# One plain feed-forward tile becomes a pair, and the second norm moves ahead of the first silu

## The chip, the core and the metric

The kernel runs on one core of a Trainium2 chip. The metric is device time in microseconds of one execution. The profile's times (us) count from the first instruction. TensorE is PE, VectorE is DVE, ScalarE is ACT, GpSimd is POOL, and SP issues most of the loads.

## The reference

One layer of a decoder for 512 prompt positions and 8 single sampled tokens, which the kernel treats as 520 columns. Cut to the part that matters:

```
x  = x + g1 * (merged @ w_out)
h2 = rms_norm(x, norm2_w) * (1 + sc2) + sh2        # mean over 1024 features, eps 1e-6
a, b = split(h2 @ w_ffn_in, 2)                     # 1024 -> 2 * 2816 (22 tiles of 128 each)
x  = x + g2 * ((silu(a) * b) @ w_ffn_out)
```

Everything is float32. Ahead of this lie a first norm, one large projection, dilated attention, a gating unit and the merge.

## The kernel before

**Layout.** Features lie on the partitions, the 520 columns on the free axis. The columns are worked on in two halves of 260. Every float32 weight tile of 128 x 1024 is split into a rounded part `hi` (an ACT copy, line 69) and a rest `lo` (a DVE subtraction, line 70), and so are the activations. A product of a weight tile with one half of the columns is 8 x 3 = 24 matmuls (`mm3`, lines 91 to 93) into one PSUM buffer of four (pool `pm`).

**Order.** The work is a list of jobs (`job`, `second_use`, `pair_job`). After each job's matmuls are written, `run` advances the side tasks by one step (`tick`, line 108: norms, sums, constants, each a generator whose `yield n` waits n ticks) and then prepares one weight tile, three tiles ahead. That order is a priority: a planner with a cost of its own for each instruction then places the instructions on each engine's queue. `behind(ins)` keeps an instruction behind a given one on its engine's queue. On the chip each engine works through its queue in that order.

**The second norm.** The last projection (`out_job`, matrix `wout`) runs over the first half's eight tiles and then the second's. `norm2(half)` squares each finished tile on ACT and adds the squares on POOL (the last on DVE). Then a matmul with ones (line 317) puts the sum over the features on every partition, and `rsqrt` computes the root with a mean on DVE (`ms`, line 878), Ln and Exp on ACT (lines 206 and 207) and three DVE steps (208 to 210), the last of which gives `rstd`. `modulate` makes from each feature tile the parts hi and lo of h2 (ACT line 296, DVE lines 294 and 297) and a whole copy for the sums (ACT line 300). The first half's norm runs beside the second half's projection, the second half's beside the first feed-forward products.

**The feed-forward tiles.** Of 22 tiles of the first feed-forward matrix, tiles 0 to 3 (`NPRE = 4`) are plain: each is four products (matrices a and b, first and second half of the columns), 96 matmuls. All the first-half products come first, then the second-half ones in the order 0, 2, 3, 1. The split weights of tiles 0, 2 and 3 are kept from the first half to the second: three of the six in a pool of their own (`khi`, `klo`, `KEPT_HOME`), three in the three ring buffers through which all weights go (`KEPT_RING`), which so prepare no other tile until their second use. Tile 1 is loaded and split twice. The silu of matrix a goes from PSUM to SBUF on ACT (line 946), and DVE multiplies it with the product of matrix b (line 949).

Tiles 4 to 21 are pairs (`pair_job`): the products of matrices a and b with both column halves are formed with seven block products of 12 matmuls (lines 994 to 996) in place of eight, 84 in all. This needs sums and differences of quarters of h2 and of the weights. `sums()` computes those of h2 on DVE (line 966, four steps), waits until the kept pool is released, and then splits three of them into the tile `tt` (line 969 on ACT, 966 on DVE). The fourth is split when the first pair runs.

**Tables.** ACT holds one set of functions at a time. `log_exp()` (line 200) asks for the set with Ln and Exp; a silu after it needs another load.

Of the kernel before, what the change touches and what calls it, by code (L numbers as in the profile page):

```python
# [13 lines left out]
AF = mybir.ActivationFunctionType  # L14
ALU = mybir.AluOpType
AX = mybir.AxisListType

P = 128
# [3 lines left out]
HT = 260  # L22
KD = 8
NFF = 22
EPS = 1e-6
# [7 lines left out]
def hybrid_layer(ctx: ExitStack, tc: tile.TileContext, io: dict):  # L33
    nc = tc.nc
    dve, act, pe, pool, sp = nc.vector, nc.scalar, nc.tensor, nc.gpsimd, nc.sync
# [13 lines left out]
    def slot(tag, name, dtype=F32, shape=(P, T)):  # L49
        return tp.tile(list(shape), dtype, tag=tag, name=name, bufs=BUFS[tag])  # L50
# [10 lines left out]
    def const(name, shape, src=None, eng=None, pl=None):  # L61
        t = (pl or cst).tile(list(shape), F32, tag=name, name=name)
        if src is not None:
            (eng or act).dma_start(out=t, in_=src)
        return t
# [17 lines left out]
    last_lo, last_mm = [None], [None]  # L83
# [107 lines left out]
    def behind(ins):  # L191

        return tc.issue_after(ins.ins) if ins else nullcontext()

    act_last = [None]
# [6 lines left out]
    def rsqrt(dst, a, tag, shape):  # L202

        y = slot(tag, "rs_y")[: shape[0], : shape[1]]
        t = slot(tag, "rs_t")[: shape[0], : shape[1]]
        act.activation(y, a, AF.Ln)
        act.activation(y, y, AF.Exp, scale=-0.5)
        dve.tensor_tensor(out=t, in0=y, in1=y, op=ALU.mult)
        dve.scalar_tensor_tensor(out=a, in0=t, scalar=-0.5, in1=a, op0=ALU.mult, op1=ALU.mult)
        return dve.scalar_tensor_tensor(out=dst, in0=a, scalar=1.5, in1=y, op0=ALU.add, op1=ALU.mult)  # L210


    cT = const("cT", (P, KD, 9), io["cT"], sp)
    ident = const("ident", (P, P))
    make_identity(nc, ident)
    ones = const("ones", (P, P))
# [164 lines left out]
    n2w = const("n2w", (P, KD))  # L381
# [13 lines left out]
    def late(out, src):  # L395

        with behind(after):
            sp.dma_start(out=out, in_=src)

    def constants():  # L400
        late(qw, io["qw"])
        late(kw, io["kw"])
        late(turns, io["turns"])
        late(lnw, io["lnw"].to_broadcast([P, 512]))
        late(lnb, io["lnb"].to_broadcast([P, 512]))
        yield 1
        with behind(last_h[0]):
            dve.tensor_scalar_mul(qw, qw, float(np.float32(128.0) ** -0.5))
        late(wsp, io["wspT"])
        late(tril, io["tril"])  # L410
        yield 3
        with behind(last_lo[0]):
            dve.tensor_tensor(out=wsp, in0=wsp, in1=tril.unsqueeze(1).to_broadcast([P, 8, P]), op=ALU.mult)
        late(bsp, io["bsp"])
        late(w00, io["w00"])
        yield 1
        late(bias0, io["bias0"])
        yield 1
        late(bias12, io["bias12"])
        late(n2w, io["n2w"])  # L420

    spawn(constants())


# [440 lines left out]
    def norm2(half):  # L865
        c = slice(half * HT, half * HT + HT)
        acc = slot("tr", "acc2", shape=(P, HT))
        for f in range(KD):
            sq = slot("tr", "sq2", shape=(P, HT)) if f else acc
            act.activation(sq, xr[f][:, c], AF.Square)  # L870
            if f:
                (pool if f + 1 < KD else dve).tensor_tensor(out=acc, in0=acc, in1=sq, op=ALU.add)
            yield 1
        tot = total(acc, "t")
        log_exp()
        rstd2 = slot("tr", "rstd2")
        ms2 = slot("tr", "ms2")
        dve.tensor_scalar(ms2[:, c], tot, 1.0 / 1024, EPS, op0=ALU.mult, op1=ALU.add)
        rsqrt(rstd2[:, c], ms2[:, c], "tr", (P, HT))
        yield 1  # L880
        if half == 0:
            h2_all.append(slots("h", "h2", 2 * KD, F32R))
            mem["ys"] = slots("ys", "g8")
            h2.extend((h2_all[0][1][f], h2_all[0][1][KD + f]) for f in range(KD))
            scales(1, 0, KD, n2w)
        else:
            modulate_samples(1, 0, KD, xr_all[0][0], rstd2, h2_all[0][0], mem["ys"][0])
        for f in range(KD):
            modulate(1, f, xr[f], rstd2, half * HT, min(half * HT + HT, TP), *h2[f],
                     mem["ys"][1][f])  # L890
            if f % 2:
                yield 1
        if half:
            spawn(sums(), 0)
# [38 lines left out]
    def ffn_job(i, which, half, place=None):  # L933

        def fn(hi=None, lo=None):
            if half == 0 and place:
                kept.halves[i, which] = hi, lo
            elif place:
                hi, lo = kept.halves.pop((i, which))
            p = product(hi, lo, h2, half)  # L940
            if half and place == "home" and not kept.halves.keys() & set(KEPT_HOME):
                kept.stack.close()
                kept.closed = True
            if which == 0:
                pend[i] = slot("tr", "silu", shape=(P, HT))
                act_last[0] = act.activation(pend[i], p, AF.Silu)
                return
            c = slice(half * HT, half * HT + HT)
            dve.tensor_tensor(out=home(i)[:, c], in0=p, in1=pend[i], op=ALU.mult)

        if half and place:
            second_use(fn, place == "ring")
        else:
            job(io["wff"][which * NFF + i], fn, home=keep if place == "home" else None, again=(place == "ring"))
# [5 lines left out]
    def sums():  # L960

        b = mem["ys"][0]
        b11, b12, b21, b22 = b[:, 0:4, 0:HT], b[:, 0:4, HT:T], b[:, 4:8, 0:HT], b[:, 4:8, HT:T]

        def minus(out, x, y):
            dve.tensor_tensor(out=out, in0=x, in1=y, op=ALU.subtract)

        def halved(hi, lo, src):
            act.activation(hi, src, AF.Copy)
            minus(lo, src, hi.bitcast(F32))  # L970


        for step in (lambda: minus(b11, b12, b11), lambda: minus(b12, b22, b12), lambda: minus(b22, b22, b11),
                     lambda: minus(b21, b21, b22)):
            with behind(last_lo[0]):
                step()
            yield 1
        while not kept.closed:
            yield 1
        tt = ctx.enter_context(tc.tile_pool(name="tt", bufs=1)).tile([P, 3, KD, HT], F32R, tag="tt", name="tt")  # L980
        mem["tt"] = tt
        for j, t in ((0, b22), (1, b12), (2, b21)):
            with behind(last_lo[0]):
                halved(tt[:, j, 0:4], tt[:, j, 4:8], t)
            yield 1
        h = h2_all[0][0]
        mem["t1"] = lambda: halved(h[:, 0:4, HT:T], h[:, KD : KD + 4, HT:T], b11)
# [124 lines left out]
                chain_[1] = dve.tensor_tensor(out=hl[1], in0=gs[k], in1=hl[0].bitcast(F32), op=ALU.subtract)  # L1112
            halved[k] = hl

    NPRE = 4
    KEPT_HOME = [(0, 0), (0, 1), (NPRE - 2, 0)]
    KEPT_RING = [(NPRE - 2, 1), (NPRE - 1, 0), (NPRE - 1, 1)]
    for half, tiles in ((0, range(NPRE)), (1, [0, NPRE - 2, NPRE - 1, *range(1, NPRE - 2)])):
# [143 lines left out]
```

## Time and profile before

| | us |
|---|---|
| median of three runs | 933.11 (932.98 to 933.7) |
| the profiled execution | 932.99 |
| its span, first to last instruction | 931.1 |
| PE busy | 909.2 (98%), 7636 matmuls |
| DVE busy | 580.4 (62%) |
| ACT busy | 414.8 (45%) |
| POOL busy | 137.6 (15%) |

The last projection's second half ends at about 571 us, the plain tiles run from 567.3 to 618.6, the pairs from there to some 800, and the down projection ends the kernel. A matmul's own record lasts about 0.28 us, as neighbours overlap; the distance between two starts is its cost. In a timeline row the bracket gives the engine's idle time before the instruction and what ended it.

### The profile page before, as it was taken

The numbers are of one execution on the slowest core, as the hardware profiler recorded it, in microseconds if no ns is written. First come the engines' busy times: TensorE is split into PE (matmuls) and PEld (weight loads), VectorE is DVE, ScalarE is ACT, GpSimd is POOL, SyncE is SP. The second block draws the span as 40 slices with busy tenths as digits, with TensorE's granted clock in tenths as the row PEclk, the third lists the DMA queues.
The fourth block names the chain that finished last, engine by engine and source line by source line (L and its number), as shares of the span: only waits on it lengthen the run. The fifth ranks groups of instructions, "written<-read, shape, count | busy, mean of one in ns | idle before, by whom it ended". The sixth has DMA issues, their size and how long they took to land.

```text
span 931.1 us, 18828 instructions
## 1 busy us (share of the span) xinstructions
PE 909.2 (98%) x7636; PEld 869.0 (93%) x7636; DVE 580.4 (62%) x1376; ACT 414.8 (45%) x818; POOL 137.6 (15%) x157
## 2 busy tenths in 40 slices
PE   3999999999999999999999999999999999999998
PEld 1799889899898989999999999999999999999998
DVE  6734675746755665643337768897888888842321
ACT  5343443443543443763333447655555555722110
POOL 0000002112102102201000322123233341000000
PEclk9999999999999999999999999999999999999999
DMA  9944436829758726645222556122332332343410
GB/s 357 361 166 132 164 114 226 272 83 309 249 178 235 244 90 176 222 129 162 92 91 92 207 180 203 47 92 92 108 121 91 98 130 92 105 146 92 126 35 24
DMA packets 41878, 142.66 MB, mean 153 GB/s; under 512 B 6328, under 2 KB 7320, under 8 KB 41792
## 3 DMA queue, kind: packets, MB, share of 16 engines
q1 hardware_dynamic: 32688, 110.14, 35.0%
q0 software_dynamic: 8608, 31.20, 11.0%
q8 instruction: 60, 0.98, 0.5%
q14 instruction: 26, 0.21, 0.1%
q10 hardware_dynamic: 496, 0.12, 0.1%
HBM read 132.81 MB, written 8.63 MB: 152 GB/s over the span
## 4 chain that ended last, share of the span: by engine, by line
PE 91%; DVE 3%; DMA 2%; ACT 2%; issue 1%; ACTq 0%; DVEq 0%; SPq 0%
PE ps L91 21%; PE ps L92 20%; PE ps L93 20%; PE pa L994 4%; PE pa L995 4%; PE pa L996 4%; PE ada L259 2%; PE pb L996 2%; PE pb L995 2%; PE pb L994 2%; PE y L672 1%; DMA wada<-wada 1%; PE ssq L524 1%; DVE lo L70 1%; PE p L996 1%
## 5 line engine op out<-in xcount | busy, mean ns | idle before, releaser
L91 PE MATMUL ps<-h,hi 128*128 128x260 f32 x1168 | 333.2, 288 | 4.0 <-ACT h L296 1.6
L93 PE MATMUL ps<-h,lo 128*128 128x260 f32 x1168 | 331.6, 285 | 0.5 <-DVE lo L70 0.5
L92 PE MATMUL ps<-h,hi 128*128 128x260 f32 x1168 | 331.3, 284 | 0.0
L70 DVE TENSOR_TENSOR lo<-raw,hi 128x1024 fp32r<-128x1024 f32 (+2 forms) x205 | 207.7, 1030 | 160.9 <-ACT hi L69 158.4
L69 ACT ACTIVATE hi<-raw 128x1024 fp32r<-128x1024 f32 (+2 forms) x205 | 170.7, 857 | 232.0 <-PE ps L92 203.1
L91 PEld LDWEIGHTS ps<-h,hi 128*128 128x128 f32 x1168 | 219.0, 189 | 16.0 <-issue 9.4
L93 PEld LDWEIGHTS ps<-h,lo 128*128 128x128 f32 x1168 | 220.3, 189 | 2.8 <-issue 1.7
L92 PEld LDWEIGHTS ps<-h,hi 128*128 128x128 f32 x1168 | 220.0, 188 | 2.8 <-issue 2.1
L1016 POOL TENSOR_TENSOR s<-raw 128x512 f32<-128x512 f32 x18 | 34.7, 1928 | 138.7 <-DMA raw<-wff 112.0
L995 PE MATMUL pb<-h,hi 128*128 128x260 f32 x144 | 40.8, 283 | 0.1
L994 PE MATMUL pa<-tt,hi 128*128 128x260 f32 x144 | 40.8, 283 | 0.1
L995 PE MATMUL pa<-tt,hi 128*128 128x260 f32 x144 | 40.8, 283 | 0.0
L996 PE MATMUL pb<-h,lo 128*128 128x260 f32 x144 | 40.8, 283 | 0.0
L994 PE MATMUL pb<-h,hi 128*128 128x260 f32 x144 | 40.7, 282 | 0.0
L996 PE MATMUL pa<-tt,lo 128*128 128x260 f32 x144 | 40.6, 282 | 0.0
L93 PE MATMUL ps<-mh,lo 128*128 128x260 f32 x128 | 36.4, 285 | 0.0
L91 PE MATMUL ps<-mh,hi 128*128 128x260 f32 x128 | 36.3, 284 | 0.0
L91 PE MATMUL ps<-gh,hi 128*128 128x260 f32 x128 | 36.3, 284 | 0.0
L92 PE MATMUL ps<-ml,hi 128*128 128x260 f32 x128 | 36.2, 283 | 0.0
L92 PE MATMUL ps<-gh,hi 128*128 128x260 f32 x128 | 36.1, 282 | 0.0
L93 PE MATMUL ps<-gh,lo 128*128 128x260 f32 x128 | 36.0, 282 | 0.0
L858 DVE SCALAR_TENSOR_TENSOR xr<-ps,mod,xr 128x260 f32<-128x260 f32 (+1 forms) x32 | 15.4, 483 | 30.7 <-PE ps L93 29.9
(280 smaller groups left out, 2000.4 us busy)
## 6 DMA issues: line engine op xcount, KB each, us to landing
raw<-win SPq DMA_DIRECT2D x60, 512.0 KB, 6.3
wada<-wada SPq DMA_DIRECT2D x48, 512.0 KB, 7.1
raw<-wff SPq DMA_DIRECT2D x46, 512.0 KB, 4.0
raw<-wout SPq DMA_DIRECT2D x16, 512.0 KB, 3.7
raw<-wfo SPq DMA_DIRECT2D x16, 512.0 KB, 3.8
kt<-ck POOLq DMA_DIRECT2D x8, 512.0 KB, 5.7
qb<-dq POOLq DMA_DIRECT2D x8, 512.0 KB, 5.5
raw<-wpj SPq DMA_DIRECT2D x8, 512.0 KB, 3.7
```

The source lines that it names most:

```text
L69: act.activation(hi, src, AF.Copy)
L70: return dve.tensor_tensor(out=lo, in0=src, in1=hi.bitcast(F32), op=ALU.subtract)
L91: pe.matmul(ps, wh, xh[:, cols], start=(first and i == 0), stop=False)
L92: pe.matmul(ps, wh, xl[:, cols], start=False, stop=False)
L93: last_mm[0] = pe.matmul(ps, wl, xh[:, cols], start=False, stop=(last and i == n - 1))
L259: last_ada[0] = pe.matmul(ps[32 * c : 32 * c + 32, :], cs[:, 4 * kh + c, :], w[:, c * 256 : c * 256 + 256], start=(kh == 0), stop=(kh == 1 ...
L524: pe.matmul(ssq[half][32 * g : 32 * g + 32, :], ones[:, 0:32], raws[g][1][:, c], start=True, stop=True, tile_position=(0, 32 * g))
L858: dve.scalar_tensor_tensor(out=dst[:, c0 : c0 + n], in0=ps[:, :n], scalar=g[:, 0:1], in1=x[:, c0 : c0 + n], op0=ALU.mult, op1=ALU.add)
L994: pe.matmul(ps, hi[:, c], xh, start=(first and k == 0), stop=False, skip_group_check=True)
L995: pe.matmul(ps, hi[:, c], xl, start=False, stop=False, skip_group_check=True)
L996: pe.matmul(ps, lo[:, c], xh, start=False, stop=(k == 3), skip_group_check=True)
L1016: pool.tensor_tensor(out=own_slot("s1", i % 2)[:, :512], in0=b[:, :512], in1=b[:, 512:], op=ALU.add)
```

## The change

`NPRE` falls from 4 to 3: tile 3 becomes the first of 19 pairs, and all six split weight tiles of tiles 0 to 2 are kept, so that none is loaded twice. A new function `rms` replaces `rsqrt` in the second norm: Ln reads the sum straight from PSUM, with scale 1/1024 and a constant bias of eps, the DVE step `ms` goes, and three DVE steps follow with a factor of -2048 left in the result, which the scaled `n2w` takes out. In the second half the sum is written with the last projection's tick, one tick earlier; every silu is queued behind the last Exp written; modulations come four to a tick, not two; and the four steps of the sums come two to a tick.

```diff
+    def rms(dst, tot, tag):
+        y = slot(tag, "rs_y", shape=(P, HT))
+        t = slot(tag, "rs_t", shape=(P, HT))
+        act.activation(y, tot, AF.Ln, scale=1.0 / 1024, bias=eps[:, 0:1])
+        exp_last[0] = act.activation(y, y, AF.Exp, scale=-0.5)
+        dve.tensor_tensor(out=t, in0=y, in1=y, op=ALU.mult)
+        dve.scalar_tensor_tensor(out=t, in0=tot, scalar=1024 * EPS, in1=t, op0=ALU.add, op1=ALU.mult)
+        return dve.scalar_tensor_tensor(out=dst, in0=t, scalar=-3072.0, in1=y, op0=ALU.add, op1=ALU.mult)
+    exp_last = [None]
...
+    eps = const("eps", (P, 1))
+    dve.memset(eps, EPS)
...
         late(n2w, io["n2w"])
+        yield 3
+        with behind(last_lo[0]):
+            dve.tensor_scalar_mul(n2w, n2w, -1.0 / 2048)
...
-            yield 1
+            if f + 1 < KD or half == 0:
+                yield 1
         tot = total(acc, "t")
         log_exp()
         rstd2 = slot("tr", "rstd2")
-        ms2 = slot("tr", "ms2")
-        dve.tensor_scalar(ms2[:, c], tot, 1.0 / 1024, EPS, op0=ALU.mult, op1=ALU.add)
-        rsqrt(rstd2[:, c], ms2[:, c], "tr", (P, HT))
+        rms(rstd2[:, c], tot, "tr")
...
-            if f % 2:
+            if f % 4 == 3:
                 yield 1
...
-                act_last[0] = act.activation(pend[i], p, AF.Silu)
+                with behind(exp_last[0]):
+                    act_last[0] = act.activation(pend[i], p, AF.Silu)
...
-        for step in (...):
+        for n, step in enumerate((...)):
             with behind(last_lo[0]):
                 step()
-            yield 1
+            if n % 2:
+                yield 1
...
-    NPRE = 4
+    NPRE = 3
     KEPT_HOME = [(0, 0), (0, 1), (NPRE - 2, 0)]
     KEPT_RING = [(NPRE - 2, 1), (NPRE - 1, 0), (NPRE - 1, 1)]
     for half, tiles in ((0, range(NPRE)), (1, [0, NPRE - 2, NPRE - 1, *range(1, NPRE - 2)])):
```

## Rows read from the trace of the kernel before

**Rows 1.** The page, busy time: us, share of the span, instructions.
```profile
PE 909.2 (98%) x7636; PEld 869.0 (93%) x7636; DVE 580.4 (62%) x1376; ACT 414.8 (45%) x818; POOL 137.6 (15%) x157
```

**Rows 2.** Busy us (instructions) by stretch: PE, PEld, DVE, ACT, POOL; clock, DMA share, GB/s.
```profile
550.00:560.00 10.00, 10.00 (x84) 9.94 (x84) 7.94 (x16) 5.91 (x10) 0.27 (x1) 1.00 0.54 166
560.00:580.00 20.00, 19.84 (x161) 19.25 (x160) 19.38 (x39) 14.38 (x28) 6.67 (x6) 1.00 0.68 224
580.00:590.00 10.00, 8.72 (x69) 8.33 (x68) 5.89 (x13) 7.61 (x10) 0.15 (x1) 1.00 0.28 87
580.00:620.00 40.00, 38.73 (x320) 38.33 (x319) 32.37 (x50) 25.60 (x46) 6.32 (x4) 1.00 0.16 56
700.00:750.00 50.00, 50.00 (x419) 50.00 (x418) 41.74 (x72) 27.72 (x56) 17.82 (x11) 1.00 0.32 106
```

**Rows 3.** Timeline of PE: start, us, line, operation, [idle before].
```profile
551.29 0.60 PE L317 MATMUL tot<-acc,ones 128*128 128x260 f32 x2
...
581.46 0.38 PE L317 MATMUL tot<-acc,ones 128*128 128x260 f32 x1
...
582.47 0.40 PE L91 MATMUL ps<-h,khi 128*128 128x260 f32 x1
...
588.25 0.28 PE L93 MATMUL ps<-h,lo 128*128 128x260 f32 x1
589.80 0.39 PE L91 MATMUL ps<-h,hi 128*128 128x260 f32 x1 [1.27 <-ACT silu L946]
```

**Rows 4.** Timeline of ACT, around both norms and the first pair.
```profile
553.30 0.40 ACT L206 ACTIVATE rs_y<-ms 128x260 f32<-128x260 f32 x1
...
560.51 0.50 ACT L296 ACTIVATE h<-modt,mod 128x260 fp32r<-128x260 f32 x1
...
582.03 0.39 ACT L946 ACTIVATE silu<-ps 128x260 f32<-128x260 f32 x1
582.43 1.28 ACT L200 ACT_TABLE_LOAD   x1
583.73 2.01 ACT L69 ACTIVATE hi<-raw 128x1024 fp32r<-128x1024 f32 x2
585.64 0.40 ACT L206 ACTIVATE rs_y<-ms 128x260 f32<-128x260 f32 x1
586.08 0.42 ACT L207 ACTIVATE rs_y<-rs_y 128x260 f32<-128x260 f32 x1
...
612.97 1.15 ACT L69 ACTIVATE hi<-raw 128x512 fp32r<-128x512 f32 x2 [1.54 <-PE ps L92]
```

**Rows 5.** Timeline of DVE, around both norms and the first pair.
```profile
551.92 0.43 DVE L878 TENSOR_SCALAR ms<-tot 128x260 f32<-128x260 f32 x1 [0.59 <-PE tot L317]
...
558.04 0.42 DVE L210 SCALAR_TENSOR_TENSOR rstd<-ms,rs_y 128x260 f32<-128x260 f32 x1
...
582.45 0.43 DVE L949 TENSOR_TENSOR g<-ps,silu 128x260 f32<-128x260 f32 x1 [2.40 <-PE ps L92]
...
588.02 0.43 DVE L210 SCALAR_TENSOR_TENSOR rstd<-ms,rs_y 128x260 f32<-128x260 f32 x1
...
598.90 0.47 DVE L297 SCALAR_TENSOR_TENSOR h<-modt,mod,h 128x252 fp32r<-128x252 f32 x1
...
605.91 2.39 DVE L966 TENSOR_TENSOR tt<-g,tt 128x1040 fp32r<-128x1040 f32 x2 [2.49 <-ACT tt L969]
...
613.63 2.39 DVE L70 TENSOR_TENSOR lo<-raw,hi 128x512 fp32r<-128x512 f32 x2
```

**Rows 6.** Groups of instructions in 580 to 620: busy us, mean ns | idle before.
```profile
L966 DVE TENSOR_TENSOR g<-g 128x1040 f32<-128x1040 f32 x4 | 4.9, 1237 | 0.1
L70 DVE TENSOR_TENSOR lo<-raw,hi 128x1024 fp32r<-128x1024 f32 x4 | 4.8, 1224 | 1.8 <-ACT hi L69 1.6
...
L69 ACT ACTIVATE hi<-raw 128x1024 fp32r<-128x1024 f32 x4 | 4.1, 1055 | 1.4 <-PE ps L92 1.4
```

**Rows 7.** Busy us (instructions) touching h2 alone, by stretch: PE, PEld, DVE, ACT; clock, DMA.
```profile
567.25:582.36 15.11, 12.34 (x96) 11.85 (x96) 2.41 (x5) 2.04 (x4) 1.00 0.56 181
```

More of the change, by code (lines that the diff above doesn't have):

```diff
@@ L970, in halved @@
             minus(lo, src, hi.bitcast(F32))
-        for step in (lambda: minus(b11, b12, b11), lambda: minus(b12, b22, b12), lambda: minus(b22, b22, b11),
-                     lambda: minus(b21, b21, b22)):
+        for n, step in enumerate((lambda: minus(b11, b12, b11), lambda: minus(b12, b22, b12),
+                                  lambda: minus(b22, b22, b11), lambda: minus(b21, b21, b22))):
             with behind(last_lo[0]):
                 step()
-            yield 1
+            if n % 2:
+                yield 1
         while not kept.closed:
```

## The prediction

> **What bounds the kernel now.** I read the page's first part, then busy time by stretch, then the PE, ACT and DVE timelines around the change. TensorE works for 98% of the span [rows 1] at the full granted clock. In the pair stage 419 matmuls start in 50 us [rows 2], one every 0.1193 us, and DVE, busy for 41.74 of those 50 us, keeps up. So time goes only where matmuls go, or where PE stands still. The one sizeable standstill near the change is in 580 to 590 us, where 69 matmuls start and 84 fit [rows 2]. It is one wait: a matmul at 588.25 us, the next at 589.80, released by a silu [rows 3].
>
> That silu was late because of ACT's tables. ACT runs the first silu at 582.03, goes back to the logarithm's table for the norm (582.43), makes two copies in 2.01 us, runs Ln and Exp, and then needs the silu table again [rows 4]: three table loads in 10 us, of which one row stands here. Four PSUM buffers hold the products, so PE cannot open another until a silu empties one.
>
> DVE is the second limit: it is busy for 7.94 us of 550 to 560, for 19.38 of 560 to 580, and for 32.37 of 580 to 620 [rows 2]. The second half of h2 is made there: its rstd begins at 588.02, its last piece at 598.90 [rows 5].
>
> **The change, part by part.** *One plain tile becomes a pair.* A plain tile costs 2 matrices x 2 halves x 24 = 96 matmuls, a pair 7 products x 12 = 84. Twelve fewer at 0.1193 us: -1.43 us, all on PE's path.
>
> It also removes four whole-tile splits from the stage before the pairs (tile 3's two and the repeated two of tile 1), ACT 1.05 and DVE 1.22 us each [rows 6], and two weight loads; the new pair's own work goes to the pair stage, whose DVE has 8.26 us left over per 50 [rows 2]. Worth nothing directly, as all this lies beside matmuls.
>
> *The stage before the pairs gets shorter.* It loses 96 matmuls, 11.5 us, while the second half's norm, modulation and the sums for the pairs stay. DVE idles 40.00 - 32.37 = 7.6 us in it now. It saves 4 x 1.22 + 2 x 0.43 (tile 3's two products with silu) + 0.43 (the ms step) = 6.2 us [rows 5, 6]. 7.6 + 6.2 - 11.5 leaves 2.3 us spare: the work fits, if its waits line up. Cost by this: 0 if they do, 2.6 us by the bound under rival 2; I take 0 because ring buffers still give each new tile two products (5.7 us) between its buffer's release and its use, and the first such split after the kept tiles shows no PE wait now.
>
> *Ln and Exp ahead of the first silu.* Two of three table loads go, the two copies of 2.01 us vanish with their tiles, and the standstill at 588.25 goes: 1.55 - 0.12 = -1.43 us [rows 3].
>
> What is late next is the first silu. Behind it stand the buffer of the first product, the later silus on ACT, and PE's fifth product. Now the fifth starts at 582.47, 0.05 us after that silu ended at 582.42 [rows 3, 4]; the four products before it ended their issue at about 582.38. In the new order the chain from the sum is: PE to reader 0.63 (551.29 to 551.92 [rows 3, 5]); Ln 0.44 (585.64 to 586.08), plus 0.10 for its bias operand (0.50 for a modulation with bias, 0.40 for Ln without [rows 4]); Exp 0.42; table 1.28; silu 0.39; hand-over 0.05. Together 3.3 us. The sum's matmul stands at 581.46, 0.92 us before 582.38. If it stays there, PE stands still 2.4 us.
>
> It should move up. In the first half, ms starts on DVE at 551.92, Ln only at 553.30 behind a weight copy, and rstd at 558.04 [rows 4, 5]. Without ms, Ln can start near 551.9, and rstd can be ready near 551.92 + 0.54 + 0.42 + 3 x 0.43 + 0.1 = 554.3, 4.1 us before its end at 558.47 now. The modulations that fill DVE in 560 to 580 [rows 2], now issued in two groups of four, can then use the 2.06 us that DVE idles in 550 to 560 [rows 2]; with ms gone, DVE should come to the last projection's residual, and through it to the sum, about 1.6 us earlier. That leaves 2.4 - 1.6 = 0.8 us of standstill. Bounds: 0 and 2.4; I take 0.8.
>
> The Trainium skill ("ScalarE: Activation LUTs", section "What ACT_TABLE_LOAD costs") charges a switch with a load of about 1283 ns and a drain of about 1380 ns. Here the silu ended at 582.42, the load began at 582.43, and the next copy at 583.73 [rows 4]: 1.30 us in all, no drain to be seen. By the page's figure the standstill would be 1.4 us more and the time about 932.6 (an estimate).
>
> *The sum with the last projection, four modulations at a time.* This fixes how early the second half of h2 is ready against its first reader. Let E be Exp's start. rstd is ready at E + 0.42 + 3 x 0.43 + 0.05, or E + 1.8. From rstd to the last piece took 598.90 + 0.47 - 588.45 = 10.9 us, with one 1.24 us sum step between [rows 5, 6]; without that step 9.7, so E + 11.5. PE resumes at E + 0.42 + 1.28 + 0.39 + 0.05 = E + 2.1, runs two products (48 x 0.1193 = 5.7) and reads the last piece 2.5 us into the next, at E + 10.4. So the last pieces are up to 1.1 us late. The cover is the next product's earlier pieces; PE's queue already crosses products over their pieces in the first half: the 96 matmuls of the first four products are spread over 15.11 us, among the last projection's [rows 7]. Bounds 0 and 1.1; I take 0.2, near the covered end.
>
> *Small edits.* The eps fill and the scaling of norm2's weights are single small DVE steps (a step of 260 columns takes 0.42 us, these have 1 and 8), the first before the first norm, the second in the stages where DVE has gaps: 0. Fewer yields in the sums change only the order. SP gains no DMA and loses two.
>
> **Sum.** -1.43 - 1.43 + 0.8 + 0.2 = -1.86 us. The profiled execution took 932.99 us (span 931.1 and 1.9 around it), the median is 933.11. 932.99 - 1.86 = 931.13; with the 0.12 to the median, 931.2.
>
> **Rivals.** *1. The first silu takes the place of the second as PE's wait.* If the instruction queues keep the sum at its place, because DVE spends the time won on weight splits (it is all but full over 560 to 580), the standstill is 2.4: -2.86 + 2.4 + 0.2 = -0.3, 932.8. For it: in the first half DVE now runs a weight split between the norm's own steps. Against it: the norm of the first half no longer passes through DVE before Ln. The table's longer price, above, belongs here as well, with 1 chance in 50.
>
> *2. Slower: DVE's waits do not fit in the shorter stage.* Place: from the sum to the first pair. DVE now waits 2.40 us for a product (582.45) and 2.49 for the copies of the transformed tiles (605.91) [rows 5]. These are dependences, not spare time. If both stay, 4.9 us of waits meet 2.3 us of spare, and 2.6 us of DVE work comes after PE wants it. A late DVE also leaves the sum where it is (2.4) and the last pieces late (1.1): -2.86 + 2.4 + 2.6 + 1.1 = +3.2, 936.3. It decides against the change from 2.9 us of new standstill on, and exceeds 0.2% from 4.7. For it: the spare is small. Against: both waits end with PE's products, and a shorter stage brings these forward too.
>
> *3. More gain.* The standstill at the first silu is 0, and PE's thin places (161 matmuls in 560 to 580 where 168 fit [rows 2]) close, since the first half's norm is early: 7 x 0.12 = 0.8 us, -2.86 - 0.8 = -3.7, 929.4. Against: those places follow weight splits, whose count there does not fall.
>
> *4. The kept halves do not do what they should.* All three ring buffers are held until the second halves, so the first pair's splits start no earlier than the first ring product ends. The first pair's first split took from 612.97 on ACT to 616.0 on DVE [rows 4, 5], 3.1 us of the 5.7 there are; with three ACT copies of about 1.05 [rows 6] ahead of it, 6.3. Price 0.6, time 931.8: inside the forecast's own range.
>
> **How the numbers follow.** Forecast (with rival 4) 50%, own range 930.0 to 932.2; rival 1 23%; rival 2 15%; rival 3 12%. Faster by over 0.2% (1.87 us, about what a measurement of this kernel can tell from no change) is 931.24 or less: a little over half of the forecast's chance, as its centre lies at that border, and rival 3: 0.41. Slower by over 0.2%: most of rival 2, which spreads from 933 up, and a rest: 0.14. Between: 0.45. The range goes from 929.4 (rival 3's time) to 934.6, which takes in rival 1 and the lower part of rival 2 and leaves out about 10% above and 5% below.
>
> **What would show it.** Right: one ACT table load between 575 and 600, Ln, Exp and then silu; no 1.5 us wait of PE after two products behind the first silu; instead a wait of 0.5 to 1.5 us ahead of the fifth product, released by silu; the first half's rstd at about 555; 12 matmuls fewer; the pair stage still at 0.1193 us. Wrong: a PE wait on pieces of h2 or on a split of the first pair longer than 1 us; more than 2 us at the first silu; a pair stage in which DVE is full.

## The result, and the profile after

The changed kernel takes 939.92 us in the median (938.73 to 940.74), the kernel before beside it on the same chip 933.6. The ratio is 1.0062, with an interval of 1.0051 to 1.0074: slower, and outside the predicted range of 929.4 to 934.6. The profiled execution took 938.78 us, its span is 937.0, against 932.99 and 931.1 before.

The page's first part for the changed kernel, busy us (share of the span) and instructions, answers to [rows 1]:

```profile
PE 909.7 (97%) x7624; PEld 869.3 (93%) x7624; DVE 582.2 (62%) x1384; ACT 413.0 (44%) x821; POOL 141.7 (15%) x159
```

The twelve matmuls are gone, as predicted, and yet PE's busy time has not fallen. Busy time by stretch tells why. The columns are those of [rows 2], and the last two rows are short stretches at the waits:

```profile
580.00:620.00 40.00, 37.22 (x284) 36.49 (x284) 32.14 (x56) 21.49 (x45) 6.00 (x6) 0.92 0.06 21
700.00:750.00 50.00, 50.00 (x419) 50.00 (x418) 41.97 (x70) 27.20 (x55) 17.95 (x10) 1.00 0.29 101
579.60:583.00 3.40, 3.33 (x14) 3.17 (x15) 3.40 (x5) 1.44 (x4) 3.40 (x4) 0.52 0.48 154
590.60:593.40 2.80, 2.80 (x13) 2.80 (x14) 2.80 (x9) 1.86 (x5) 0.00 (x0) 0.50 0.02 6
```

In 580 to 620 only 284 matmuls start, where 320 did before, and the granted clock is 0.92 of full speed. The loss sits at two waits of PE, each with a short stretch at about half clock, the 1.2 GHz level, behind it. The pair stage (700 to 750) is as before, to the matmul.

PE's timeline shows both (start, us, line, operation, [idle before <- what ended it]):

```profile
577.62 0.28 PE L91 MATMUL ps<-h,khi 128*128 128x260 f32 x1
579.67 0.54 PE L92 MATMUL ps<-h,khi 128*128 128x260 f32 x1 [1.77 <-DVE h L311]
...
583.05 0.34 PE L91 MATMUL ps<-h,khi 128*128 128x260 f32 x1
...
587.08 0.28 PE L93 MATMUL ps<-h,lo 128*128 128x260 f32 x1
587.20 0.60 PE L331 MATMUL tot<-acc,ones 128*128 128x260 f32 x2
590.58 0.59 PE L91 MATMUL ps<-h,hi 128*128 128x260 f32 x1 [2.78 <-ACT silu L963]
...
593.34 0.32 PE L91 MATMUL ps<-h,hi 128*128 128x260 f32 x1
...
597.82 0.39 PE L91 MATMUL ps<-h,khi 128*128 128x260 f32 x1
```

From the first matmul on h2 (568.71; 567.30 before) to the fifth product (590.58; 582.47 before) it takes 21.87 us, 6.70 more than before [rows 3, 7]. Three terms make it up. A wait of 2.05 us for a piece of h2: 1.93 over a normal step. Fourteen matmuls at half clock, 579.67 to 583.05: 3.38 - 14 x 0.1193 = 1.71. The wait for the first silu, 587.20 to 590.58 without the sum's own two passes of 0.12: 3.14. Together 6.78. Behind it twelve more matmuls run at half clock, 2.76 us for 1.43, so that the 1.43 which the old standstill gives back is not to be seen; the section on the clock asks what that stretch costs.

The balance is best made from the first matmul on h2 to the end of the span, 363.80 us before and 368.29 after, since single profiles reach that matmul anywhere between 567.2 and 570.1. Kernels with the same order of instructions ahead of it (the changed one and the one with PE kept busy, below) reach it at 568.71 and 570.06. The stage up to the first pair takes 46.35 instead of 51.34 - 11.45 (a plain tile), +6.46. The rest takes 321.94 instead of 312.46: 9.48 for a pair, 0.54 less than 84 x 0.1193. With the twelve matmuls, +6.46 - 0.54 - 1.43 = +4.49. The remaining 1.4 of the 5.9 between the two spans lie ahead of h2. They look like scatter: PE's order is the same with three and with four tiles in the new order up to 24 matmuls ahead of that one. But all nine profiles with three tiles reach it later (568.2 to 570.1) than four of the five with four tiles (567.2 to 567.9; the fifth 569.1), so whether a part belongs to the change stays open.

ACT's timeline shows that the new order did what it says, one table load in place of three:

```profile
587.89 0.48 ACT L216 ACTIVATE rs_y<-tot,eps 128x260 f32<-128x260 f32 x1 [2.50 <-PE tot L331]
588.40 0.42 ACT L217 ACTIVATE rs_y<-rs_y 128x260 f32<-128x260 f32 x1
588.84 1.28 ACT L963 ACT_TABLE_LOAD   x1
590.13 0.39 ACT L963 ACTIVATE silu<-ps 128x260 f32<-128x260 f32 x1
```

From the sum at 587.20 to PE's resumption is 3.38 us, a chain in which nothing waits. The prediction made it 3.3. It only began too late. Two things set its start: when the squares' sum `acc` is ready on DVE, and where the sum's matmul stands on PE's queue. In the kernel before the last addition on DVE was this one:

```profile
579.62 0.43 DVE L872 TENSOR_TENSOR acc<-acc,sq 128x260 f32<-128x260 f32 x1 [0.62 <-ACT sq L870]
```

It ended at 580.05, and the sum's matmul started at 581.46: with its operand ready, it stood 1.41 us in PE's queue (the shortest such distance in these runs is 0.21). In the changed kernel that addition (586.19, below) ends at 586.62, 17.9 us after the first matmul on h2 where before it took 12.75, and the matmul follows 0.58 us later, behind all 96 matmuls of the first four products.

POOL and DVE show the other half, the reason for the late operand: work that the prediction did not look for here. Their timelines, POOL first:

```profile
574.44 1.64 POOL L1034 TENSOR_TENSOR s<-raw 128x512 f32<-128x512 f32 x1 [4.34 <-DMA raw<-wff]
576.16 1.50 POOL L1035 TENSOR_TENSOR raw<-raw 128x512 f32<-128x512 f32 x1
577.63 1.71 POOL L889 TENSOR_TENSOR acc<-acc,sq 128x260 f32<-128x260 f32 x1
579.29 1.47 POOL L1034 TENSOR_TENSOR s<-raw 128x512 f32<-128x512 f32 x1
580.72 0.74 POOL L889 TENSOR_TENSOR acc<-acc,sq 128x260 f32<-128x260 f32 x1
581.41 1.46 POOL L1035 TENSOR_TENSOR raw<-raw 128x512 f32<-128x512 f32 x1
```

```profile
574.85 1.25 DVE L880 TENSOR_TENSOR xr<-rt,xr 128x8 f32<-128x8 f32 x1
...
576.43 0.47 DVE L875 SCALAR_TENSOR_TENSOR xr<-ps,mod,xr 128x252 f32<-128x252 f32 x1
576.82 1.92 DVE L70 TENSOR_TENSOR lo<-raw,hi 128x1024 fp32r<-128x1024 f32 x1
578.67 0.95 DVE L311 SCALAR_TENSOR_TENSOR h<-modt,mod,h 128x260 fp32r<-128x260 f32 x1
579.54 1.24 DVE L880 TENSOR_TENSOR xr<-rt,xr 128x8 f32<-128x8 f32 x1
580.71 1.04 DVE L311 SCALAR_TENSOR_TENSOR h<-modt,mod,h 128x260 fp32r<-128x260 f32 x1
581.74 1.42 DVE L311 SCALAR_TENSOR_TENSOR h<-modt,mod,h 128x260 fp32r<-128x260 f32 x1
...
586.19 0.43 DVE L889 TENSOR_TENSOR acc<-acc,sq 128x260 f32<-128x260 f32 x1 [0.64 <-POOL acc L889]
```

Lines 1034 and 1035 are the sums of the first two pairs' weight quarters. Before, the first of them ran at 589.85, after the norm. With one plain tile fewer the pairs' weights are loaded that much earlier, and POOL takes them up between the norm's own adds. Beside POOL's steps, DVE steps that read two operands from SBUF take longer: 0.95 to 1.42 us for 0.48, 1.92 for 1.21, 1.25 for 0.15. The step that reads one operand from PSUM (`xr<-ps`, 576.43) keeps its 0.47 beside POOL's second step.

### The profile page after: what moved, and what is told of

Its sections match the earlier page's. It is cut to its first block, busy times and chain, and to the rows that moved or that the text cites. A ratio compares the mean times of both kernels' runs of the same rounds, so it can differ in the third digit from the quotient of the medians.

```text
span 937.0 us, 18807 instructions
## 1 busy us (share of the span) xinstructions
PE 909.7 (97%) x7624; PEld 869.3 (93%) x7624; DVE 582.2 (62%) x1384; ACT 413.0 (44%) x821; POOL 141.7 (15%) x159
## 4 chain that ended last, share of the span: by engine, by line
PE 91%; DMA 3%; DVE 3%; ACT 1%; issue 1%; SPq 0%; DVEq 0%; ACTq 0%; POOLq 0%
PE ps L91 21%; PE ps L92 20%; PE ps L93 20%; PE pa L1013 4%; PE pa L1014 4%; PE pa L1012 4%; PE pb L1014 2%; PE pb L1013 2%; PE pb L1012 2%; PE ada L273 2%; PE y L689 1%; DMA wada<-wada 1%; PE ssq L541 1%; PE p L1013 1%; PE p L1014 1%; PE p L1012 1%
## 5 line engine op out<-in xcount | busy, mean ns | idle before, releaser
L91 PE MATMUL ps<-h,hi 128*128 128x260 f32 x1136 | 324.3, 288 | 5.8 <-ACT silu L963 2.8
L93 PE MATMUL ps<-h,lo 128*128 128x260 f32 x1136 | 322.4, 285 | 0.6 <-DVE lo L70 0.6
L92 PE MATMUL ps<-h,hi 128*128 128x260 f32 x1136 | 322.5, 285 | 0.3 <-DVE h L311 0.3
L70 DVE TENSOR_TENSOR lo<-raw,hi 128x1024 fp32r<-128x1024 f32 (+2 forms) x206 | 205.0, 1014 | 158.4 <-ACT hi L69 156.1
L91 PEld LDWEIGHTS ps<-h,hi 128*128 128x128 f32 x1136 | 213.5, 189 | 17.4 <-issue 9.1
L92 PEld LDWEIGHTS ps<-h,hi 128*128 128x128 f32 x1136 | 214.3, 189 | 3.3 <-issue 2.1
L93 PEld LDWEIGHTS ps<-h,lo 128*128 128x128 f32 x1136 | 214.4, 189 | 2.8 <-issue 1.7
L1034 POOL TENSOR_TENSOR s<-raw 128x512 f32<-128x512 f32 x19 | 37.6, 1981 | 144.3 <-DMA raw<-wff 104.4
L1013 PE MATMUL pa<-tt,hi 128*128 128x260 f32 x152 | 43.1, 283 | 0.0
L1014 PE MATMUL pb<-h,lo 128*128 128x260 f32 x152 | 43.0, 283 | 0.0
L1012 PE MATMUL pb<-h,hi 128*128 128x260 f32 x152 | 43.0, 283 | 0.0
L1012 PE MATMUL pa<-tt,hi 128*128 128x260 f32 x152 | 42.9, 283 | 0.0
L1013 PE MATMUL pb<-h,hi 128*128 128x260 f32 x152 | 42.9, 282 | 0.0
L1014 PE MATMUL pa<-tt,lo 128*128 128x260 f32 x152 | 42.8, 282 | 0.0
```

The costliest lines, as they stand in the source:

```text
L70: return dve.tensor_tensor(out=lo, in0=src, in1=hi.bitcast(F32), op=ALU.subtract)
L91: pe.matmul(ps, wh, xh[:, cols], start=(first and i == 0), stop=False)
L92: pe.matmul(ps, wh, xl[:, cols], start=False, stop=False)
L93: last_mm[0] = pe.matmul(ps, wl, xh[:, cols], start=False, stop=(last and i == n - 1))
L1012: pe.matmul(ps, hi[:, c], xh, start=(first and k == 0), stop=False, skip_group_check=True)
L1013: pe.matmul(ps, hi[:, c], xl, start=False, stop=False, skip_group_check=True)
```

## The experiments

Every ratio is to the kernel before on the same chip. The last column is the time from the first matmul on h2 to the end of the span, from one profile each (363.80 before, 368.29 after); that one execution can lie up to 3.5 us from the kernel's median (943.18 and 939.70 for the one with PE kept busy).

| kernel | ratio, interval | us |
|---|---|---|
| four tiles, old order | 0.9995, 0.9985 to 1.0006 | 363.74 |
| four tiles, new order | 1.0045, 1.0030 to 1.0061 | 368.41 |
| three tiles, old order | 1.0095, 1.0069 to 1.0120 | 373.67 |
| after: three tiles, new order | 1.0062, 1.0051 to 1.0074 | 368.29 |
| pairs' POOL sums behind the norm's adds | 1.0035, 1.0019 to 1.0051 | 368.35 |
| the same, early pair splits too | 1.0031, 1.0018 to 1.0044 | 366.24 |
| norm's second adds on DVE | 1.0054, 1.0036 to 1.0072 | 369.01 |
| before, with POOL steps added | 0.9994, 0.9983 to 1.0004 | 362.79 |
| PE kept busy at the silu | 1.0075, 1.0040 to 1.0109 | 371.34 |
| three tiles, silus copied out | 1.0048, 1.0029 to 1.0066 | 366.53 |
| four tiles, silus copied out, samples first | 1.0020, 1.0006 to 1.0033 | 364.75 |
| three tiles, silus copied out, samples first | 1.0062, 1.0045 to 1.0079 | 367.92 |
| the same, POOL sums last | 1.0022, 1.0012 to 1.0031 | 365.41 |

### The norm's new order, and the third tile, apart

The first kernel keeps the whole change but the tile; the second also takes back the sum's tick and the silus' place behind Exp; the third does that with three tiles.

```diff
-    NPRE = 3
+    NPRE = 4
```

> The changed kernel with four plain tiles as before: the norm's part of the change alone. Theory A: no pair's sum comes into the norm, since the pairs' weights come later; the wait of 1.43 us for the second silu goes, that at the first silu stands instead with 0 to 2.4 us: 932.5 to 934.5. Theory B: 2.4 us or more at the first silu, with the clock at half behind it: 935 to 937. Theory C says nothing of it: 932 to 934.

```diff
-            if f + 1 < KD or half == 0:
-                yield 1
+            yield 1
...
-                with behind(exp_last[0]):
-                    act_last[0] = act.activation(pend[i], p, AF.Silu)
+                act_last[0] = act.activation(pend[i], p, AF.Silu)
...
-    NPRE = 3
+    NPRE = 4
```

> Four plain tiles, the new rms and the modulations four at a time, but the sum is written one tick later as before and the silu is not queued behind Exp, so the first silu stands ahead of Ln and Exp again with three table loads. Theory B, the silu order, now put so: the sum's matmul comes only when TensorE has used up its four buffers, and the chain sum, Ln, Exp, table, silu of 3.3 us stands whole in TensorE's way, with a stretch at half clock behind it; then this run loses that wait, has the wait of about 1.4 us for the second silu in its place, and takes 933 to 934.5, some 4 us less than with the new order (937.97). Rival: the new rms or the grouping of the modulations is what costs; then it stays at 936.5 to 938.

> The changed kernel with three plain tiles, the sum written one tick later as before and the silu not queued behind Exp; the early GpSimd sums of the pairs stay. Theory B: the wait of 3.4 us ahead of the fifth product goes, a wait of 1.4 us or more for the second silu comes, and what the GpSimd sums cost stays: 936 to 938. Theory A alone (GpSimd's queue is the whole loss): 939 to 940.

Measured: the new order alone makes four tiles slower (1.0045), and taking it back gives the time of before (0.9995) with the new `rms` still in. So `rms`, its DVE step fewer and the regrouped modulations are worth nothing by themselves, and the order costs 4.7 us (0.0050 x 934); how much of it the tick costs and how much the silus' place is not shown. The third tile alone costs more still: 1.0095 against 0.9995, 9.3 us. The two costs overlap, since their sum is far more than the 5.8 of both (0.0062 x 934). Two of the three came out above all that was expected of them: the new order with four tiles at 937.97, three tiles in the old order at 942.46. PE's timeline of four tiles in the new order, and busy time in the stretch behind it:

```profile
581.98 0.60 PE L331 MATMUL tot<-acc,ones 128*128 128x260 f32 x2
582.22 0.47 PE L93 MATMUL ps<-h,lo 128*128 128x260 f32 x1
585.80 0.59 PE L91 MATMUL ps<-h,khi 128*128 128x260 f32 x1 [3.11 <-ACT silu L963]
```

```profile
585.80:590.90 5.10, 5.10 (x23) 5.10 (x24) 5.10 (x11) 2.99 (x8) 2.62 (x2) 0.50 0.24 90
```

The first POOL sum of a pair runs at 585.36 here, so it has no part in this wait. The squares' sum is ready on DVE at 580.22, and its matmul starts only at 581.98, with one matmul of the four products left. So PE stands still for 3.58 us behind the silu's chain (a weight copy stands ahead of Ln in it), with 24 matmuls at half clock behind that: 5.10 us, 2.2 too many. The same place in the old order, where the first silu ran at 581.16, ahead of Ln:

```profile
589.40 0.39 PE L91 MATMUL ps<-h,hi 128*128 128x260 f32 x1 [0.56 <-ACT silu L961]
596.16 0.39 PE L91 MATMUL ps<-h,khi 128*128 128x260 f32 x1 [0.72 <-ACT silu L961]
```

Three table loads and two waits of 0.85 and 1.00 us from start to start, none followed by a lower clock, cost far less than one open chain. With three tiles in the old order PE waits elsewhere:

```profile
582.02 0.39 PE L92 MATMUL ps<-h,khi 128*128 128x260 f32 x1 [1.75 <-DVE h L311]
584.15 0.59 PE L92 MATMUL ps<-h,khi 128*128 128x260 f32 x1 [0.77 <-DVE h L311]
...
602.42 0.80 PE L91 MATMUL ps<-h,khi 128*128 128x260 f32 x2 [4.40 <-ACT h L69]
```

The first two are pieces of h2's first half, delayed as in the changed kernel. The last are the samples' columns of its second half, which reach PE only after 4.68 us. The logarithm starts late (the sum at 594.29), and three tiles then leave too few products to cover the second half's norm. The new order, in which no wait of this length is left there, gains 3.1 us at three tiles.

### POOL's sums

First, the first two pairs' sums behind the norm's last POOL add:

```diff
+            with behind(last_add[0] if i < NPRE + 2 else None):
                 pool.tensor_tensor(out=own_slot("s1", i % 2)[:, :512], in0=b[:, :512], in1=b[:, 512:], op=ALU.add)
                 pool.tensor_tensor(out=b[:, :512], in0=a[:, :512], in1=b[:, :512], op=ALU.subtract)
```

> The changed kernel, but the GpSimd sums of the first two pairs' weights (two per pair) are queued behind the norm's last GpSimd addition. Theory A, GpSimd's queue: these four steps (1.64, 1.50, 1.47 and 1.46 us) stand between the additions of the second half's squares and also stretch VectorE's steps beside them; put behind, the wait of 2.05 us for a piece of h2 goes, the sum's matmul comes 4 to 5 us earlier, the wait at the first silu falls from 3.4 to under 1.5 us, and the time to about 934 (5 to 6 us less). Theory B, the silu order: the sum comes earlier but TensorE still waits 2.4 us or more for the first silu, and the time is 936 to 937. Theory C, the stage is too short for VectorE whatever the order: no change, 939 to 940.

DVE's timeline in the stretch in which its steps were long:

```profile
576.59 1.21 DVE L70 TENSOR_TENSOR lo<-raw,hi 128x1024 fp32r<-128x1024 f32 x1
577.73 0.48 DVE L311 SCALAR_TENSOR_TENSOR h<-modt,mod,h 128x260 fp32r<-128x260 f32 x1
578.13 0.71 DVE L880 TENSOR_TENSOR xr<-rt,xr 128x8 f32<-128x8 f32 x1
```

The steps have their length of before, the wait of 2.05 us and the half clock after it are gone, and the last matmul of the fourth product starts at 584.01, 3.5 us sooner when counted from the first matmul on h2. The silu's wait stays (584.13 to 587.46, then half clock). About 2 us of the median come back (937.82), less than either theory wanted. The profiled execution (939.61) shows little of it: the POOL sums now run from 582.35 to 588.4, and the two splits behind them (line 70, 583.85) take 3.42 us for what takes 1.36 at the free rate of 0.68, with a further wait of 2.25 us at 594.54.

Next, those splits too, behind Exp and DVE's last add:

```diff
+            with behind(exp_last[0] if early_pair else None), behind(last_add[1] if early_pair else None):
                 split(own_slot("ah", i % 2)[:, :512], own_slot("al", i % 2)[:, :512], b[:, 512:])
```

> As the run before, and the split of the fourth combination (ah, al) of the first two pairs is also queued behind the norm: its copy behind Exp, its subtraction behind VectorE's last addition. Theory A: the two subtractions (1.23 and 0.68 us) that stood ahead of the last residual step and of the last addition go, the sum comes another 1 to 1.5 us earlier, the time is about 933. Theory B: as the run before, 936. Theory C: 939 to 940.

Median much the same (936.98, 1.0031), and the silu's wait is now the largest single one, 583.83 to 588.19: the splits' two copies, put behind Exp, stand ahead of the table load on ACT (585.31 to 586.44). Next, POOL's sums left early and the second half's adds moved from POOL to DVE:

```diff
-                (pool if f + 1 < KD else dve).tensor_tensor(out=acc, in0=acc, in1=sq, op=ALU.add)
+                (pool if f + 1 < KD and half == 0 else dve).tensor_tensor(out=acc, in0=acc, in1=sq, op=ALU.add)
```

> The changed kernel, but all additions of the second half's squares run on VectorE; the pairs' GpSimd sums stay as early as they are. This parts the two ways in which GpSimd can hurt. If it is only that the additions wait in GpSimd's queue, the sum comes about 3 us earlier and the time is 935 to 936. If it is mostly that GpSimd's steps stretch VectorE's beside them, VectorE's steps between 575 and 584 us stay at twice their length, the wait of 2 us for a piece of h2 stays, and the time is 938 to 940. Theory C: 940 or more, for 5 x 0.43 us more on VectorE.

```profile
580.03 0.39 PE L92 MATMUL ps<-h,khi 128*128 128x260 f32 x1 [2.70 <-DVE h L311]
```

```profile
578.50 1.48 DVE L311 SCALAR_TENSOR_TENSOR h<-modt,mod,h 128x260 fp32r<-128x260 f32 x1
```

With nothing of the norm queued behind POOL's sums the wait for h2 stays, 2.98 us, DVE's step for that piece takes 1.48 us for 0.48, and the sum comes only 0.5 us earlier, counted from the first matmul on h2 (17.97 us for 18.48). So POOL hurts through DVE, and its queue is the smaller part. Last, the kernel before with eight unused POOL steps of 112 columns among the norm's adds:

```diff
+            for _ in range(2 if half and 2 <= f < 6 else 0):
+                pool.tensor_tensor(out=idle, in0=acc[:, :112], in1=acc[:, :112], op=ALU.add)
```

> The kernel before with nothing changed but eight additional POOL steps (112 columns each, their result unused), two behind each of four adds of the second half's norm, where in the changed kernel the pairs' POOL steps stand. DVE's and ACT's queues are as before. Theory A (POOL's steps delay the norm by themselves, through POOL's queue and by stretching DVE steps beside them): the eight take about 0.7 to 0.9 us each, the sum's matmul comes 2 us or more later than 581.46, DVE steps of 0.45 us beside them show 0.9 or more, PE waits 1 to 3 us more in 575 to 592, and the time is 934.5 to 937. Theory B (only the new order of table, Ln, Exp and silu costs time, POOL's steps lie beside matmuls): within 0.2% of before, 933 to 934.5.

The time is that of before. The sum comes 15.05 us after the first matmul on h2, 0.9 later than before, and not the 2 that the first theory wanted. In the old order silu does not hang on it, and PE's wait for the second silu even falls from 1.55 to 0.41 us. So POOL's steps are no cost in themselves; these are shorter, too, than the pairs' sums. They cost where a product waits for the DVE step beside them.

### The clock

Twelve unused passes of PE (six products of the ones with the squares' sum) behind the norm's sum:

```diff
+        if half:
+            idle = bank("t", "idle", (P, HT))
+            for _ in range(6):
+                pe.matmul(idle, ones, acc, start=True, stop=True)
```

> The changed kernel; behind the second half's sum TensorE makes the same product with ones six times more into a buffer that nobody reads, which fills about 3.0 of the 3.4 us in which it waits for the first silu. If the halved clock after 590 us comes from TensorE having stood still, the next dozen matmuls start every 0.12 us and not every 0.22: 1.2 to 1.4 us less, 938.5 against 939.9. If it has another cause, the pace stays at 0.22 and the time at 939.9.

```profile
592.05 2.79 PE L896 MATMUL idle<-acc,ones 128*128 128x260 f32 x12
595.00 0.39 PE L91 MATMUL ps<-h,hi 128*128 128x260 f32 x1
...
602.24 0.39 PE L91 MATMUL ps<-h,khi 128*128 128x260 f32 x1 [1.23 <-ACT silu L967]
```

```profile
595.00:600.70 5.70, 5.70 (x47) 5.70 (x48) 5.70 (x17) 4.74 (x14) 0.00 (x0) 1.00 0.00 0
```

The 48 matmuls after the silu take 5.74 us at full clock; in the changed kernel they take 7.01. So the lower clock behind that wait comes from the standstill: 1.3 us over these 48 matmuls. But it is not a cost in the total here. The next product starts 7.25 us after the first in both kernels (595.00 to 602.24; 590.58 to 597.82): at full clock PE stands still for 1.51 us behind a later silu on ACT, and at half clock that wait is filled. So the median stays at 939.70, the value that the other reading gave. The profiled execution (943.18) is longer still, as its waits for h2 ahead of the sum were 1.32, 2.02 and 1.05 us, with half clock behind the last.

### Trying to keep the gain

The POOL sums and the early splits stay behind the norm, as above, and the sum is written one tick later again, as in the kernel before. The products of the first two silus are copied out of PSUM by ACT, and silu works on the copies behind Exp:

```diff
+                if half == 0 and i < 2:
+                    src = pend[i]
+                    act.activation(src, p, AF.Copy)
```

> Three plain tiles, the pairs' early work on GpSimd, ScalarE and VectorE queued behind the norm as in the second run, and the products of the first two silus copied out of PSUM by ScalarE's Copy, which needs no table; the silus are then taken from the copies behind Exp. Theory B: the fifth product no longer waits for the table load; a wait of up to 1 us is left ahead of the sixth, there is no stretch at half clock, and the time falls by 3.5 to 5 us against the second run (936.98), to 932 to 933.5. Theory C: the time won comes back as waits for the second half of h2 or for the first pair's tiles: 935.5 to 937.

```profile
593.55 0.50 PE L91 MATMUL ps<-h,khi 128*128 128x260 f32 x2 [2.70 <-ACT h L69]
594.76 0.39 PE L92 MATMUL ps<-h,khi 128*128 128x260 f32 x1 [0.70 <-DVE h L70]
```

The wait of 3.4 us ahead of the fifth product is gone, and the ratio is 1.0048 (937.30) all the same, a little above the second theory: PE runs into the second half of h2 instead, 2.98 and 1.21 us, with fifteen matmuls at half clock from 596.12 on. The next two put the samples' columns first, the pairs' POOL sums behind rstd and their early splits behind the last modulation, for four tiles and for three:

```diff
+            last_add[0] = pool.tensor_tensor(out=eps2, in0=rstd2[:, HT : HT + 1], in1=rstd2[:, HT : HT + 1], op=ALU.add)
...
+                     mem["ys"][1][f], sample_ops if half else (None, None, None))
```

> The same with four plain tiles. Theory B: with the products copied out, Ln and Exp ahead of the first silu cost nothing, one table load is left of three, and the waits for silus (1.55 us in the kernel before) go; the longer stage leaves no wait for h2: 931.5 to 932.5, against 933.7 before and 937.97 for the norm part alone. If the stage's length is what matters and not the silu: 933.5 to 934.5.

> The run with the copied products, three plain tiles, and three changes of order behind the norm: the samples' eight columns of h2, which the first second-half matmul reads, come ahead of the other modulations; the early split of the first two pairs' fourth combination comes behind the last modulation; the pairs' GpSimd sums wait for rstd. The run before stood 2.98 and 1.21 us for the samples' columns, had a stretch at half clock of some 2.6 us behind that, and its rstd came 3.9 us after Exp's start where 1.8 would do. If that, the lateness of the second half of h2 in a stage that is 11.5 us shorter, is what is left of the loss: rstd 2 us earlier, the waits under 1.5 us in all, no half clock, 932 to 933.5. If the loss only moves on to the first pair's tiles (their GpSimd sums are later now): 935 to 937.

Both missed their expectations: four tiles with 935.31, where PE waits 1.00, 0.93 and 1.06 us for products that DVE and ACT empty, and three tiles with 939.58, 6 us above the first theory and 2.6 above the second. The DVE timeline of three tiles, and after it the row of POOL's first sum:

```profile
589.47 1.31 DVE L331 TENSOR_TENSOR mods<-mods,amod 128x64 f32<-128x64 f32 x1
590.82 1.19 DVE L332 TENSOR_TENSOR mods<-mods,mod 128x64 f32<-128x64 f32 x1
591.94 3.29 DVE L310 SCALAR_TENSOR_TENSOR modt<-xr,amod,rstd 128x252 f32<-128x252 f32 x3
```

```profile
589.18 1.52 POOL L1056 TENSOR_TENSOR s<-raw 128x512 f32<-128x512 f32 x1
```

POOL's four sums run here from 589.18 to 594.55, right beside the second half's modulations. A DVE step of 64 columns begins at 589.47 and ends at 590.78, 0.08 us after POOL's first step (590.70). The next ends at 592.01, the same distance after the second. DVE and POOL take turns here. So the last kernel moves POOL's sums behind the last modulated piece:

```diff
+            end = h2[KD - 1][1][:, TP - 1 : TP].bitcast(F32)
+            pgate[0] = pool.tensor_tensor(out=eps2, in0=end, in1=end, op=ALU.add)
...
+            with behind(pgate[0]):
```

> Three tiles, the first two silus copied out of PSUM, the samples' columns first, and now the first two pairs' POOL sums (four steps of about 1.5 us) only behind the last piece of the second half of h2, so that no POOL step lies beside the modulations. Theory A (in the kernel without this edit POOL's steps at 589.18 to 594.55 stretched the modulations beside them): the DVE steps of 0.95 to 1.3 us there fall to about 0.45, the wait of 2.90 us for h2 falls below 1, no stretch at half clock follows it, and the time is 934 to 936. Theory B (the stage is too short for DVE's work whatever stands beside it): the waits for h2 stay together near 4 us or move to the first pair's splits or to the sums for the pairs, and the time stays at 937 to 940.

```profile
590.31 0.22 DVE L332 TENSOR_TENSOR mods<-mods,amod 128x64 f32<-128x64 f32 x1
590.56 0.22 DVE L333 TENSOR_TENSOR mods<-mods,mod 128x64 f32<-128x64 f32 x1
590.70 1.26 DVE L310 SCALAR_TENSOR_TENSOR modt<-xr,amod,rstd 128x252 f32<-128x252 f32 x3
```

The same steps: 0.22 for 1.31 and 1.19, 1.26 for 3.29. The largest wait for h2 is 1.23 us, the clock is 1.00 throughout, and the time falls to 936.28, 3.3 us below the kernel without this edit. That is the first theory, 0.3 above its bound. It is still slower than before, by 1.6 us from the first matmul on h2 on: the stage up to the first pair has come down to 41.46 us, but POOL's sums, now beside DVE's sums for the pairs, end only at 610.4, and at the first pair PE waits three times for DVE, 0.47, 0.95 and 0.69 us between 611 and 618. Whether another place for the four sums would bring these back was not tried. No version here beats the kernel before.

## Why the prediction was wrong

**The step that failed** is "It should move up", with its "0.8 us of standstill". The standstill at the first silu was 3.38 us. The chain was sized right (3.3 predicted, 3.38 measured); its start was not. The prediction let the sum follow DVE's work and so come earlier. But already in the kernel before the sum did not wait for DVE: its operand was ready at 580.05 and its matmul stood in PE's queue until 581.46. In the changed kernel the planner put it behind all 96 matmuls of the first four products, four matmuls further back than before, so that not even the 0.92 us that lay between the sum and the last of these matmuls remained. With four tiles in the new order, where no POOL sum of a pair runs so early, the operand is ready 1.76 us ahead of the matmul, PE still stands still for 3.58 us, and the ratio is 1.0045. In the changed kernel itself the queue holds the sum for only 0.58 us: there its operand, too, is late, by the second failure below. The half clock behind the silu did not add to the price, as far as the one profile with PE kept busy shows.

**The first half's rstd** was to be ready at about 555, 4.1 us earlier. It was ready at 559.54, 6.34 us after its own sum (553.20); before it took 7.18, so it came 0.84 us earlier. Ln was early, but Exp stood behind a weight copy and the DVE steps behind splits. A wait that is removed ahead of one instruction is given back when the next stands behind other work on the same queue.

**"Worth nothing directly, as all this lies beside matmuls"**, about the new pair's own work, was the second failure, one of place. The pair's POOL sums do not run in the pair stage; they run when their weights land, 574.44 us, in the middle of the norm. The prediction counted DVE's steps at their mean lengths and never asked what ran beside them. The trace of before had the sign: POOL's first pair sums at 589.85 stand beside modulations of 1.18 and 1.32 us. Price in the changed kernel: 2.05 us of wait and 1.7 of half clock ahead of the sum, and an operand that was ready 5.2 us later, counted from the first matmul on h2. These do not add up with the silu's wait, which comes behind both; the sums put behind the norm gave back about 2 us of the median, and in the last pair of kernels, with the silus copied out, 3.3. The Trainium skill ("SBUF — State Buffer", section "Who interferes with whom") says that a DVE instruction with two SBUF inputs contends with a GpSimd instruction that reads SBUF, and calls the ports that they share an exclusive lock. The trace agrees: 1.31 us for a step of 0.22 that ended 0.08 us after POOL's, and 0.47 for the one with an operand in PSUM.

**The clock** had no term. In the profile before it was 1.00 beside the only long wait, of 1.55 us; nothing there priced a longer one.

**The second half's last pieces** (0.2, bound 1.1) cost nothing to be seen in the changed kernel, where PE was late itself. With the silus copied out PE came to the second half's first pieces earlier and stood 2.98 and 1.21 us: the cover that the prediction counted on was not there.

**The rivals.** The first (the silu takes the place of the old wait, 932.8) named the right wait with 2.4 us for 3.38, and left out what follows on it. The second (936.3) had the right sign, half the size (+3.2 us for +6.3) and not the mechanism. Its place was from the sum to the first pair, and there DVE idled 6.6 of 27.9 us (21.23 busy, 587.20 to 615.06), so it was not full; less the 4.5 us lost at the silu, that is close to the 2.3 us of spare time worked out. DVE was stretched ahead of the sum, where the prediction did not look.

**Right:** twelve matmuls, one table load at 1.28 us, the pair stage's pace, no wait of the first pair for a kept ring buffer, and small edits at nothing (0.9995 in the old order at four tiles).

## What to carry to other kernels

A chain that is moved ahead of a PSUM reader has to begin before the products that fill the buffers end; look up where its first instruction will stand on each queue and whether it already waits there with its operand ready, and price the chain whole if it comes last. When a stage is shortened, list which engines' loads and sums move forward with it, and what they will stand beside: the lengths of DVE steps with two SBUF operands, measured where POOL is idle, did not hold beside POOL.

## What the hardware showed unexpectedly

DVE steps with two SBUF operands beside POOL's 512-column steps took 0.95 to 1.42 us instead of 0.48, and 1.2 to 1.3 instead of 0.15 or 0.22. After standstills of PE of 2.05, 3.38 and 3.58 us the granted clock was about 0.50 for 3.4, 2.8 and 5.1 us; after those of 1.55 (before), 0.85 and 1.00 it stayed at 1.00, and also after one of 2.98 us (norm's second adds on DVE, 1.00 from 580.03 to 586.2). After one of 4.36 us (early pair splits too) twelve matmuls ran at full pace first, 588.19 to 589.75, and then fifteen at 0.22 us each: the loss need not follow right on the wait, and the length of the wait alone does not tell whether one comes.
